# Macaron block on one core: VectorE's order of weight sums, a chunked output projection, and a norm sum one product later

## The chip, the cores and the metric

The kernel runs on one core of a Trainium2 chip. The metric is the device time of one execution in microseconds (us). The engines are TensorE (PE, matrix products; its weight loads are listed as PEld), VectorE (DVE), ScalarE (ACT), GpSimd (POOL) and SyncE (SP), which issues the loads from memory. Each engine works through its own queue in a fixed order and waits for others by semaphores.

## The reference

A transformer block in the macaron form, one batch of 512 tokens, width 1024, in float32:

```python
x = x + 0.5 * swiglu(rmsnorm(x, g1), wg1, wu1, wd1)      # first FFN, hidden 2816
y = rmsnorm(x, g_mix) @ w_in                             # q, k, v, gates of 16 heads
o = concat(moba_attention(8 heads), nsa_attention(8 heads))
x = x + o @ w_out                                        # output projection
x = x + 0.5 * swiglu(rmsnorm(x, g2), wg2, wu2, wd2)      # second FFN
z = rmsnorm(x, gf)
# swiglu(h) = (silu(h @ w_gate) * (h @ w_up)) @ w_down
```

MoBA chooses key blocks of 256 by their mean key; NSA mixes compressed, chosen and windowed keys by three gates. Both add a relative position bias.

## The kernel before

**Layout and precision.** Activations lie transposed: `xs[d]` is block d of 128 features by 512 tokens, d = 0 to 7. A product is made to nearly float32 precision from halves: each operand is split into hi (ACT copies it to the short type) and lo (DVE or POOL subtracts hi), and `mm3` (L99 to L102) issues three matmuls: hi x hi (L100), lo x hi (L101), hi x lo (L102). `halves` (L76 to L96) splits weights into `whi` (L91, ACT) and `wlo` (L95 on DVE, or L93 on POOL).

**FFN.** Class `Ffn` (L187) holds 22 hidden blocks. The first four are "plain": 24 matmuls of 512 columns for gate and 24 for up; `finish` (L281 to L283) multiplies both by R, the reciprocal norm of each token, and `kept` (L250 to L255) splits the result into the halves called `h`. The other 18 go in nine pairs by Winograd's form of Strassen's product: seven products for gate and seven for up, 12 matmuls of 256 columns each. Their weight blocks come as tiles `aw`, sums S1 to S4 of these are made on DVE (`sums`, L303), halves `sph` and `spl` of blocks and sums by `halves_of_x` (L226 ACT, L227 DVE), and the results are put together at L327 to L349 (`t`). The same Strassen form needs sums of the activations (`sums_of_x`, L211 to L224: `xa` to `xd`, halves `th`, `tl`; `blocks_of_x`: `xo`). `down` (L375 to L402) makes the down product of up to four hidden blocks (`pd`), whose banks `half_added` (L487) adds to `x`. `lay` (L411) lists steps and runs each product's loads 12 steps ahead, its sums 6 and its halves 4.

**What sets the order.** A scheduler lays down each engine's order from the program's order and its own model of times; `tc.issue_after(i)` makes it put the instructions of a block behind instruction i on their engine. With `behind_rms = (f, m)` the matmuls of product m of plain block f go behind the matmuls `pr` that sum the squares (L175); `pR` (L181) then hands out the reciprocal norm, and ACT copies it to R (L182).

**Output projection.** It is fill work for the attention: `stream` loads jobs three ahead from a pool of four buffers and PE gets their matmuls between those of the attention. A job of `w_out` (L766 to L778) takes one block d and two of the four pairs of heads. The attention's head leaves its bank `po` by `out_halves` (L805 to L823): ACT copies hi (L819), DVE makes `to` (L820), ACT copies `u` (L822), POOL adds both to lo (L823). The lines of `oT` for pairs 0 to 3 are named `kvn` in the trace.

Of the kernel before, what the change touches and what calls it, by code (L numbers as in the profile page):

```python
# [16 lines left out]
D = 1024  # L17
# [4 lines left out]
FP = 4  # L22
# [7 lines left out]
def block_kernel(ctx: ExitStack, tc: tile.TileContext, A: dict, out: bass.AP):  # L30
# [156 lines left out]
    class Ffn:  # L187
# [14 lines left out]
        def __init__(self, wg, wu, which, tmp, hp, sp):  # L202
            self.w, self.which, self.tmp, self.hp, self.sp = (wg, wu), which, tmp, hp, sp
            self.xg, self.hs, self.steps = None, {}, []
            self.b, self.temps = {}, {}
            self.behind_rms = None
            self.th, self.tl = [sp.tile([128, 4, 3, HT], F32R, name=n, tag=n, bufs=1) for n in ("th3", "tl3")]
            sp.tile([128, 16], F32, name="gap", tag="gap", bufs=1)
# [15 lines left out]

        def halves_of_x(self, hi, lo, v):
            nc.scalar.activation(hi, v, AF.Copy)  # L226
            nc.vector.tensor_tensor(lo, v, f32(hi), ALU.subtract)  # L227

        def blocks_of_x(self, k):
            a, b, c = self.temps.pop(k)  # L230
# [58 lines left out]
        def pair(self, f):  # L289
# [8 lines left out]
            def sums(m, name):  # L298

                a11, a12, a21, a22 = [A[m, i, j] for i in range(2) for j in range(2)]  # L300
                to, x, y, op = {"S1": (a21, a21, a22, ALU.add), "S2": (a11, a21, a11, ALU.add),
                                "S3": (a21, a11, a22, ALU.subtract), "S4": (a12, a11, a12, ALU.add)}[name]
                nc.vector.tensor_tensor(to, x, y, op)  # L303

            def halves_of(m, name):
                i, j = {"A11": (0, 0), "A12": (0, 1), "S1": (1, 0), "S2": (0, 0), "S3": (1, 0), "S4": (0, 1),
# [59 lines left out]
                                  lambda m=m, then=then: then(m)])  # L366
            return steps

        def down(self, w, fs, then, tag="mm", groups=(1,) * NK):

            n = len(fs)
            raw, got, bank = {}, {}, {}

            def loads(d):
                if d % (8 // n) == 0:  # L375
                    raw[d * n // 8] = chunk((8, 128))
                    fetch(raw[d * n // 8], w[d * n // 8])

            def halves_of(d):
                if d % (4 // n) == 0:  # L380
                    i = d * n % 8
                    for k, v in enumerate(halves(raw[d * n // 8][:, i:i + 4])):
                        got[d + k // n, k % n] = v

            def run(d):
                ds = {sum(groups[:g]): range(sum(groups[:g]), sum(groups[:g + 1])) for g in range(len(groups))}.get(d)
                if ds is None:
                    return
                for i in ds:
                    bank[i] = pt(tag, "pd")  # L390
                for ks in ([range(n)] if len(ds) == 1 else [range(n - 1), range(n - 1, n)]):
                    for i in ds:
                        for k in ks:
                            mm3(bank[i], got[i, k], self.hs[fs[k]], k == 0, k == n - 1)
                for i in ds:
                    then(i, bank[i])

            return [[lambda d=d: loads(d), None, lambda d=d: halves_of(d), lambda d=d: run(d), None, True]
                    for d in range(NK)]

# [10 lines left out]
        def lay(self, wd):  # L411

            for f in range(FP):
                self.steps += self.plain(f)
            self.steps += self.down(wd[0], range(FP), half_added, None, (4, 4))
            fills = []
            for f in range(FP, NF, FP):
                fs = range(f, min(f + FP, NF))
                pairs = [step for i in fs[::2] for step in self.pair(i)]
                self.steps += self.mixed(pairs, fills) if fills else pairs  # L420
                if len(fs) == FP:
                    fills = self.down(wd[f // FP], fs, half_added)
# [128 lines left out]
    with ExitStack() as ph:  # L551
# [211 lines left out]
        oT = {}  # L763
        out_done = set()

        def w_out(d, k0, k1):  # L766
            def body(w):
                while any(2 * k + 1 not in out_done for k in range(k0, k1)):
                    yield
                p = pt("mm", "pw")  # L770
                for k in range(k0, k1):
                    mm3(p, w[k - k0], oT[k], k == k0, k == k1 - 1)
                    yield
                nc.vector.tensor_tensor(xs[d], p, xs[d], ALU.add)
                if k1 == 4:
                    got["x", d] = gained(d, 2)
                    squares(tmp, d, "t", 6)
            return A["w_o"][d][:, k0:k1], body  # L778

        def stream(jobs, ahead=3):  # L780

# [24 lines left out]
        def out_halves(h):  # L806
# [13 lines left out]
            nc.vector.tensor_tensor(t[b], o[:64], f32(hi[b]), ALU.subtract)  # L820
            u = tmp.tile([128, S], F32, name="u", tag="t", bufs=6)
            nc.scalar.activation(u[b], o[64:], AF.Copy)  # L822
            nc.gpsimd.tensor_tensor(lo[b], t[b], u[b], ALU.add)  # L823

        QIS = ((0, 1), (2,), (3,))
        JS = ((0,), (1,), (2, 3))
# [143 lines left out]
        for i in range(4):  # L970
            fill += [proj(2 * i, moba_t("q", i)), proj(2 * i + 1, moba_t("k", i))]
            if i == 2:
                fill += [w_out(d, 4, 6) for d in range(NK)]
        fill += [w_out(d, k, k + 2) for k in (6, 0) for d in range(NK)]
        last = [w_out(d, 2, 4) for d in range(NK)]
        work = stream(pre + fill + last)
        done = [0]

# [60 lines left out]
    with ExitStack() as ph:  # L1039
# [2 lines left out]
        sp = ph.enter_context(tc.tile_pool(name="sp3", bufs=2))  # L1042
        ffn = Ffn(A["wg2"], A["wu2"], 2, tmp, hp, sp)
        ffn.xg = xg
        ffn.behind_rms = 1, 0
        hs = ffn.hs

        def after(i):
# [93 lines left out]
def _laid_out(x, norm_ffn1, w_ffn1_gate, w_ffn1_up, w_ffn1_down, norm_mix, w_in, cmp_pos_k, cmp_w1_k,  # L1142
# [19 lines left out]
        "w1": np.stack([kp(cmp_w1_k[0]), kp(cmp_w1_v[0])]),  # L1162
        "w2": np.stack([kp(cmp_w2_k[0]), kp(cmp_w2_v[0])]),
        "pos": c(cat([pos, pos], axis=0)),
        "w_o": _blocks(w_out[0], D, 128),
        "wg2": _blocks(w_ffn2_gate[0], D, 128), "wu2": _blocks(w_ffn2_up[0], D, 128),
        "wd2a": _down(w_ffn2_down[0])[0],
        "wd2b": _blocks(w_ffn2_down[0][F - F % (FP * 128):], F % (FP * 128), S),
# [26 lines left out]
```

## Time and profile before

| | us |
|---|---|
| median of 3 runs | 1009.53 (1008.88 to 1009.92) |
| profiled execution | 1011.25 |
| its span | 1009.5 |
| PE busy | 983.8 |
| DVE busy | 776.9 |
| ACT busy | 564.9 |
| POOL busy | 137.3 |

The span runs from the first to the last instruction of the profiled execution; the rest of its time lies around it. The page's row of PE's granted clock, in tenths for 40 slices, reads 9 in all but the last (8). A busy PE is not a PE at its peak, since matmuls overlap; where PE stands still is seen in the waits and in the starts of its matmuls. The stages in order of time: first FFN to about 360 us, projections and attention to 636, the rest of the output projection to about 655 with the second FFN's first products among it, second FFN and last norm to the end.

### The profile page before, as it was taken

The page shows a single profiled execution, that of the slowest core. Times are in us where ns is not written, and L with a number is a line of the kernel's source. Part 1 is how long each engine was busy: PE and PEld are TensorE (multiplying, and loading weights), DVE is VectorE, ACT ScalarE, POOL GpSimd, SP SyncE. Part 2 cuts the span into 40 slices and gives each one's busy share as a digit, 9 for nine tenths or more (in the row PEclk, how much of TensorE's full clock was granted, in tenths as well). Part 3 has the DMA queues.
Part 4 walks back from the last instruction along what each step waited for, and adds up shares of the span by engine and source line. Part 5 has one row for each costly group of instructions (what it writes and reads, how often), then busy time and mean ns, then how long its engine had stood idle before and what let it go on. Part 6 is the DMA issues. An engine that isn't in the chain of part 4 may idle for free.

```text
span 1009.5 us, 17013 instructions
## 1 busy us (share of the span) xinstructions
PE 983.8 (97%) x6080; PEld 871.0 (86%) x6080; DVE 776.9 (77%) x1578; ACT 564.9 (56%) x1181; POOL 137.3 (14%) x193
## 2 busy tenths in 40 slices
PE   8999999999999999999999999999999999999996
PEld 6779999999999898787878888788899999999995
DVE  6797888788766488758888978779878888776744
ACT  6463654454444266557677977655455445444436
POOL 0000000000000000036555776300000000000002
PEclk9999999999999999999999999999999999999998
DMA  7254544233501125541011322425244232341102
GB/s 244 87 197 153 186 149 113 98 101 89 161 25 54 45 85 177 165 127 38 20 45 32 93 65 84 140 86 209 69 144 142 86 105 91 120 146 43 33 11 84
DMA packets 53513, 104.53 MB, mean 104 GB/s; under 512 B 10513, under 2 KB 19170, under 8 KB 53428
## 3 DMA queue, kind: packets, MB, share of 16 engines
q1 hardware_dynamic: 53428, 103.44, 32.6%
q8 instruction: 48, 0.79, 0.3%
q14 instruction: 37, 0.30, 0.1%
HBM read 97.98 MB, written 5.30 MB: 102 GB/s over the span
## 4 chain that ended last, share of the span: by engine, by line
PE 82%; DVE 11%; DMA 3%; issue 2%; ACT 1%; POOL 0%; SPq 0%; DVEq 0%; ACTq 0%; POOLq 0%
PE pd L102 6%; PE pd L100 6%; PE pd L101 6%; PE pu L100 6%; PE pu L102 5%; PE pu L101 5%; PE pw L100 4%; PE pw L101 4%; PE pw L102 4%; PE pp L102 3%; PE pgu L100 3%; PE pp L100 3%; PE pp L101 3%; PE pgu L101 3%; PE pv L100 3%; PE pgu L102 3%
## 5 line engine op out<-in xcount | busy, mean ns | idle before, releaser
L226 ACT ACTIVATE sph<-aw 128x512 fp32r<-128x512 f32 x252 | 155.7, 628 | 138.0 <-PE pu L101 68.1
L91 ACT ACTIVATE whi<-raw 128x512 fp32r<-128x512 f32 (+2 forms) x216 | 124.6, 589 | 151.3 <-PE pd L101 71.8
L227 DVE TENSOR_TENSOR spl<-aw,sph 128x512 fp32r<-128x512 f32 x252 | 170.0, 685 | 49.5 <-ACT sph L226 47.9
L101 PE MATMUL pd<-h,whi 128*128 128x512 f32 x336 | 131.9, 392 | 1.4 <-DVE h L255 1.4
L102 PE MATMUL pd<-h,wlo 128*128 128x512 f32 x336 | 130.9, 390 | 0.8 <-DVE wlo L95 0.6
L95 DVE TENSOR_TENSOR wlo<-raw,whi 128x512 fp32r<-128x512 f32 (+1 forms) x168 | 110.9, 671 | 23.9 <-ACT whi L91 22.6
L100 PE MATMUL pd<-h,whi 128*128 128x512 f32 x336 | 129.0, 392 | 0.0
L100 PE MATMUL pu<-th,sph 128*128 128x256 f32 x432 | 121.5, 281 | 1.1 <-DVE t L339 1.1
L303 DVE TENSOR_TENSOR aw<-aw 128x512 f32<-128x512 f32 x144 | 97.6, 683 | 31.7 <-DMA aw<-in_wg 13.6
L102 PE MATMUL pu<-th,spl 128*128 128x256 f32 x432 | 121.1, 280 | 0.0
L101 PE MATMUL pu<-tl,sph 128*128 128x256 f32 x432 | 121.0, 280 | 0.0
L487 DVE SCALAR_TENSOR_TENSOR x<-pd,x 128x512 f32<-128x512 f32 x88 | 59.9, 685 | 44.7 <-PE pd L102 44.4
L100 PEld LDWEIGHTS pu<-th,sph 128*128 128x128 f32 x432 | 81.6, 189 | 2.8 <-DVE t L339 1.3
L101 PEld LDWEIGHTS pu<-tl,sph 128*128 128x128 f32 x432 | 81.9, 190 | 1.1
L100 PE MATMUL pw<-xo,sph 128*128 128x256 f32 x288 | 80.8, 281 | 0.8 <-DVE x L487 0.5
L102 PEld LDWEIGHTS pu<-th,spl 128*128 128x128 f32 x432 | 81.2, 188 | 0.1
L101 PE MATMUL pw<-xo,sph 128*128 128x256 f32 x288 | 80.4, 280 | 0.0
L102 PE MATMUL pw<-xo,spl 128*128 128x256 f32 x288 | 79.7, 280 | 0.0
L102 PEld LDWEIGHTS pd<-h,wlo 128*128 128x128 f32 x336 | 63.1, 188 | 14.1 <-DVE wlo L95 1.2
L101 PEld LDWEIGHTS pd<-h,whi 128*128 128x128 f32 x336 | 63.3, 188 | 12.8 <-DVE h L255 2.2
L100 PEld LDWEIGHTS pd<-h,whi 128*128 128x128 f32 x336 | 62.9, 188 | 11.1
L100 PEld LDWEIGHTS pw<-xo,sph 128*128 128x128 f32 x288 | 54.1, 188 | 2.6 <-ACT sph L226 1.6
(245 smaller groups left out, 2454.5 us busy)
## 6 DMA issues: line engine op xcount, KB each, us to landing
aw<-in_wg SPq DMA_DIRECT2D x72, 256.0 KB, 3.8
aw<-in_wu SPq DMA_DIRECT2D x72, 256.0 KB, 3.6
raw<-in_wd1a SPq DMA_DIRECT2D x20, 512.0 KB, 4.7
raw<-in_wd2a SPq DMA_DIRECT2D x20, 512.0 KB, 4.8
raw<-in_w_a SPq DMA_DIRECT2D x16, 512.0 KB, 4.4
raw<-in_w SPq DMA_DIRECT2D x8, 512.0 KB, 3.7
raw<-in_w_o SPq DMA_DIRECT2D x32, 128.0 KB, 2.2
raw<-in_wg SPq DMA_DIRECT2D x7, 512.0 KB, 3.8
```

What stands on the lines that cost most here:

```text
L91: nc.scalar.activation(hi, v, AF.Copy)
L95: nc.vector.tensor_tensor(lo, v, f32(hi), ALU.subtract)
L100: nc.tensor.matmul(p, w[0], v[0], start=first, stop=False, skip_group_check=again)
L101: nc.tensor.matmul(p, w[0], v[1], start=False, stop=False, skip_group_check=again)
L102: nc.tensor.matmul(p, w[1], v[0], start=False, stop=last, skip_group_check=again)
L226: nc.scalar.activation(hi, v, AF.Copy)
L227: nc.vector.tensor_tensor(lo, v, f32(hi), ALU.subtract)
L303: nc.vector.tensor_tensor(to, x, y, op)
L487: nc.vector.scalar_tensor_tensor(xs[d], p, 0.5, xs[d], ALU.mult, ALU.add)
```

## The change

Four edits:

1. `halves_of_x` remembers the last `lo` it issued. The sums S1 to S4 on DVE, and the split of the down weights, go behind the newest one (`behind_lo`). The first down part of each FFN is left out (`kept_back=False`) as far as its weights are concerned.
2. `w_out` takes four blocks and two pairs of heads at a time: 8 jobs with a load of 512 KB and two splits of 128x512 instead of 32 jobs with 128 KB and one split of 128x256. The last two jobs hold four banks (two of tag `mm`, two of `s`) and make the products of pair 2 of all four before those of pair 3. The weights' layout follows.
3. For the last head, 7, the final add of `out_halves` is on DVE instead of POOL.
4. `behind_rms` of the second FFN is (1, 1) instead of (1, 0).

```diff
         def halves_of_x(self, hi, lo, v):
             nc.scalar.activation(hi, v, AF.Copy)
-            nc.vector.tensor_tensor(lo, v, f32(hi), ALU.subtract)
+            self.last_lo = nc.vector.tensor_tensor(lo, v, f32(hi), ALU.subtract)
+
+        def behind_lo(self):
+            return tc.issue_after(self.last_lo.ins) if self.last_lo else nullcontext()
...
-                nc.vector.tensor_tensor(to, x, y, op)
+                with self.behind_lo():
+                    nc.vector.tensor_tensor(to, x, y, op)
...
-        def down(self, w, fs, then, tag="mm", groups=(1,) * NK):
+        def down(self, w, fs, then, tag="mm", groups=(1,) * NK, kept_back=True):
...
-                    for k, v in enumerate(halves(raw[d * n // 8][:, i:i + 4])):
+                    with self.behind_lo() if kept_back else nullcontext():
+                        parts = halves(raw[d * n // 8][:, i:i + 4])
+                    for k, v in enumerate(parts):
...
-            self.steps += self.down(wd[0], range(FP), half_added, None, (4, 4))
+            self.steps += self.down(wd[0], range(FP), half_added, None, (4, 4), False)
...
-        def w_out(d, k0, k1):
+        def w_out(g, k0, last=False):
             def body(w):
-                while any(2 * k + 1 not in out_done for k in range(k0, k1)):
+                while any(2 * k + 1 not in out_done for k in (k0, k0 + 1)):
                     yield
-                p = pt("mm", "pw")
-                for k in range(k0, k1):
-                    mm3(p, w[k - k0], oT[k], k == k0, k == k1 - 1)
+                ps = {}
+                for i, k in [(i, k) for k in range(2) for i in range(4)] if last else [
+                        (i, k) for i in range(4) for k in range(2)]:
+                    if k == 0:
+                        ps[i] = pt("mm" if not last or i < 2 else "s", "pw")
+                    mm3(ps[i], w[2 * i + k], oT[k0 + k], k == 0, k == 1)
                     yield
-                nc.vector.tensor_tensor(xs[d], p, xs[d], ALU.add)
-                if k1 == 4:
-                    got["x", d] = gained(d, 2)
-                    squares(tmp, d, "t", 6)
-            return A["w_o"][d][:, k0:k1], body
+                    if k == 1:
+                        d = 4 * g + i
+                        nc.vector.tensor_tensor(xs[d], ps[i], xs[d], ALU.add)
+                        if last:
+                            got["x", d] = gained(d, 2)
+                            squares(tmp, d, "t", 6)
+            return A["w_o"][k0 // 2, g], body
...
-            nc.gpsimd.tensor_tensor(lo[b], t[b], u[b], ALU.add)
+            (nc.vector if h == 7 else nc.gpsimd).tensor_tensor(lo[b], t[b], u[b], ALU.add)
...
-                fill += [w_out(d, 4, 6) for d in range(NK)]
-        fill += [w_out(d, k, k + 2) for k in (6, 0) for d in range(NK)]
-        last = [w_out(d, 2, 4) for d in range(NK)]
+                fill += [w_out(g, 4) for g in range(2)]
+        fill += [w_out(g, k) for k in (6, 0) for g in range(2)]
+        last = [w_out(g, 2, True) for g in range(2)]
...
-        ffn.behind_rms = 1, 0
+        ffn.behind_rms = 1, 1
```

The change shifts the lines: of the new kernel, L228 is L227 of before, L309 is L303, L260 is L255, L288 is L283, L218, L219 and L221 are L217, L218 and L220, L495 is L487, L788 is L774, L834 and L838 are L820 and L823.

What the edits do to the order, at three places. First, DVE in the first FFN, ahead of the `h` of the fourth plain block; before:

```order
L283 TENSOR_TENSOR t<-t 128x512
L303 TENSOR_TENSOR aw<-aw 128x512
L217 TENSOR_TENSOR xc<-xa 128x256
L227 TENSOR_TENSOR xo<-xa,xo 128x256
L303 TENSOR_TENSOR aw<-aw 128x512
L227 TENSOR_TENSOR xo<-xb,xo 128x512
L255 TENSOR_TENSOR h<-t,h 128x512
```

And now:

```order
L288 TENSOR_TENSOR t<-t 128x512
L218 TENSOR_TENSOR xc<-xa 128x256
L228 TENSOR_TENSOR xo<-xa,xo 128x256
L228 TENSOR_TENSOR xo<-xb,xo 128x512
L219 SCALAR_TENSOR_TENSOR xd<-xc,xb 128x256
L221 TENSOR_TENSOR xa<-xb,xa 128x256
L228 TENSOR_TENSOR spl<-aw,sph 128x512 x2
L309 TENSOR_TENSOR aw<-aw 128x512
L228 TENSOR_TENSOR spl<-aw,sph 128x512
L260 TENSOR_TENSOR h<-t,h 128x512
```

The sums (`aw<-aw`) have gone from between the block sums, two more of them from just above these rows; three `spl`, one sum and two pieces of `sums_of_x` stand ahead of `h` that stood behind it.

Second, PE after the last matmul of the attention (`po`); before, `kvn_7522` is the lo of the last pair of heads, which `out_halves` makes last:

```order
L107 MATMUL po_7529<-tl_7514,vm_4844 128x128
L100 MATMUL pw_7764<-kvn_7421,whi_7718 128x512
L101 MATMUL pw_7764<-kvn_7422,whi_7718 128x512
L102 MATMUL pw_7764<-kvn_7421,wlo_7719 128x512
L100 MATMUL pw_7783<-kvn_7421,whi_7732 128x512
L101 MATMUL pw_7783<-kvn_7422,whi_7732 128x512
L102 MATMUL pw_7783<-kvn_7421,wlo_7733 128x512
L100 MATMUL pw_7764<-kvn_7521,whi_7718 128x512
L100 MATMUL pw_7783<-kvn_7521,whi_7732 128x512
L101 MATMUL pw_7764<-kvn_7522,whi_7718 128x512
```

Now six matmuls of another block follow the last `po`, then these rows; `kvn_7510` is the lo of the last pair:

```order
L100 MATMUL pw_7676<-kvn_7409,whi_7562 128x512
L101 MATMUL pw_7676<-kvn_7410,whi_7562 128x512
L102 MATMUL pw_7676<-kvn_7409,wlo_7563 128x512
L100 MATMUL pw_7676<-kvn_7509,whi_7562 128x512
L100 MATMUL pw_7684<-kvn_7509,whi_7566 128x512
L100 MATMUL pw_7688<-kvn_7509,whi_7566 128x512
L100 MATMUL pw_7680<-kvn_7409,whi_7562 128x512
L101 MATMUL pw_7680<-kvn_7410,whi_7562 128x512
L102 MATMUL pw_7680<-kvn_7409,wlo_7563 128x512
L100 MATMUL pw_7680<-kvn_7509,whi_7562 128x512
L101 MATMUL pw_7676<-kvn_7510,whi_7562 128x512
```

Eight matmuls stood between the last `po` and the first that needs the last lo; sixteen stand there now, in four banks. On DVE the last lo is made here, behind an `x` add and the `wlo` of the second FFN's first weights:

```order
L834 TENSOR_TENSOR to<-po,kvn 64x512
L788 TENSOR_TENSOR x_91<-pw,x_91 128x512
L95 TENSOR_TENSOR wlo<-raw,whi 128x512
L838 TENSOR_TENSOR kvn<-to,u 64x512
L788 TENSOR_TENSOR x_72<-pw,x_72 128x512
```

Before, `kvn<-to,u` stood on POOL, with nothing of another kind behind `to` on DVE but the next `x` adds.

Third, DVE in the second FFN around the `h` of the fourth plain block and the first add of the down part; before:

```order
L303 TENSOR_TENSOR aw<-aw 128x512
L218 SCALAR_TENSOR_TENSOR xd<-xc,xb 128x256
L220 TENSOR_TENSOR xa<-xb,xa 128x256
L227 TENSOR_TENSOR spl<-aw,sph 128x512 x4
L227 TENSOR_TENSOR xo<-xc,xo 128x256
L255 TENSOR_TENSOR h<-t,h 128x512
L219 SCALAR_TENSOR_TENSOR xd<-xd,xb 128x256
L227 TENSOR_TENSOR tl_7919<-xa,th_7918 128x256
L303 TENSOR_TENSOR aw<-aw 128x512 x2
L227 TENSOR_TENSOR spl<-aw,sph 128x512
L227 TENSOR_TENSOR tl_7919<-xd,th_7918 128x512
L487 SCALAR_TENSOR_TENSOR x_72<-pd,x_72 128x512
```

And now:

```order
L260 TENSOR_TENSOR h<-t,h 128x512
L219 SCALAR_TENSOR_TENSOR xd<-xc,xb 128x256
L221 TENSOR_TENSOR xa<-xb,xa 128x256
L228 TENSOR_TENSOR spl<-aw,sph 128x512 x2
L309 TENSOR_TENSOR aw<-aw 128x512
L228 TENSOR_TENSOR spl<-aw,sph 128x512
L309 TENSOR_TENSOR aw<-aw 128x512
L228 TENSOR_TENSOR xo<-xc,xo 128x256
L228 TENSOR_TENSOR spl<-aw,sph 128x512
L220 SCALAR_TENSOR_TENSOR xd<-xd,xb 128x256
L495 SCALAR_TENSOR_TENSOR x_72<-pd,x_72 128x512
```

The `spl` and the sums have gone from ahead of `h` to behind it, and stand between `h` and the first `x`.

## Rows read from the trace of the kernel before

**Rows 1.** The page: busy time, share of the span and number of instructions of each engine; then the chain of work that ended last, its shares by engine.

```profile
PE 983.8 (97%) x6080; PEld 871.0 (86%) x6080; DVE 776.9 (77%) x1578; ACT 564.9 (56%) x1181; POOL 137.3 (14%) x193
...
PE 82%; DVE 11%; DMA 3%; issue 2%; ACT 1%; POOL 0%; SPq 0%; DVEq 0%; ACTq 0%; POOLq 0%
```

**Rows 2.** Timeline of PE in the first down part: start, duration (of all that are grouped), engine, line, operation, number, and in brackets the idle time before it and what ended it.

```profile
67.30 1.07 PE L100 MATMUL pd<-h,whi 128*128 128x512 f32 x4
68.69 0.50 PE L101 MATMUL pd<-h,whi 128*128 128x512 f32 x1 [0.32 <-DVE h L255]
```

**Rows 3.** Waits of PE from 60 to 105 us: what waited for what, us in total, times, longest.

```profile
PE pu L100 <- DVE t L339: 1.1, 1, 1.1
PE pd L102 <- DVE wlo L95: 0.6, 1, 0.6
PE pw L100 <- DVE x L487: 0.5, 1, 0.5
PE pd L101 <- DVE h L255: 0.3, 1, 0.3
```

**Rows 4.** Waits of PE from 636 to 650 us.

```profile
PE pw L101 <- POOL kvn L823: 1.6, 1, 1.6
PE pw L100 <- DVE x L774: 0.8, 2, 0.5
```

**Rows 5.** Waits of PE from 700 to 800 us.

```profile
PE pd L101 <- DVE h L255: 1.1, 1, 1.1
PE pv L100 <- ACT sph L226: 0.9, 1, 0.9
PE pv L102 <- DVE spl L227: 0.3, 1, 0.3
PE pw L100 <- ACT sph L226: 0.3, 1, 0.3
PE pu L100 <- DVE t L348: 0.3, 1, 0.3
```

**Rows 6.** Timeline of DVE in the first FFN, 60.5 to 75 us.

```profile
61.20 0.67 DVE L303 TENSOR_TENSOR aw<-aw 128x512 f32<-128x512 f32 x1
...
66.76 0.67 DVE L303 TENSOR_TENSOR aw<-aw 128x512 f32<-128x512 f32 x1
...
67.96 0.67 DVE L255 TENSOR_TENSOR h<-t,h 128x512 fp32r<-128x512 f32 x1
...
72.31 1.27 DVE L487 SCALAR_TENSOR_TENSOR x<-pd,x 128x512 f32<-128x512 f32 x2
73.51 0.67 DVE L95 TENSOR_TENSOR wlo<-raw,whi 128x512 fp32r<-128x512 f32 x1
```

**Rows 7.** The page's DMA issues: tile and source, queue, number, KB each, us from issue to landing.

```profile
raw<-in_w_a SPq DMA_DIRECT2D x16, 512.0 KB, 4.4
...
raw<-in_w_o SPq DMA_DIRECT2D x32, 128.0 KB, 2.2
```

**Rows 8.** Groups of POOL's instructions by form: line, operation, shape, number, busy us, mean ns of one, idle before and its releasers.

```profile
L93 POOL TENSOR_TENSOR wlo<-raw,whi 128x256 fp32r<-128x256 f32 x32 | 24.8, 780 | 10.6 <-ACT whi L91 9.1 <-PE pw L101 1.1
L93 POOL TENSOR_TENSOR wlo<-raw,whi 128x512 fp32r<-128x512 f32 x16 | 21.2, 1324 | 4.0 <-ACT whi L91 4.0
```

**Rows 9.** Timeline of all engines at the end of the attention, 636 to 640 us.

```profile
636.00 0.28 PE L107 MATMUL po<-tl,vm 128*128 128x128 f32 x1
...
636.31 0.59 ACT L819 ACTIVATE kvn<-po 64x512 fp32r<-64x512 f32 x1 [0.17 <-PE po L107]
...
637.01 0.68 DVE L820 TENSOR_TENSOR to<-po,kvn 64x512 f32<-64x512 f32 x1 [0.41 <-POOL wlo L93]
...
637.73 0.59 ACT L822 ACTIVATE u<-po 64x512 f32<-64x512 f32 x1 [0.82 <-DVE to L820]
638.46 1.26 POOL L823 TENSOR_TENSOR kvn<-to,u 64x512 fp32r<-64x512 f32 x1 [1.49 <-ACT u L822]
...
639.77 0.50 PE L101 MATMUL pw<-kvn,whi 128*128 128x512 f32 x1 [1.60 <-POOL kvn L823]
```

**Rows 10.** One line of DVE, L595, a subtraction of two tensors in SBUF: number, duration in ns (least, median, most), first and last start. POOL has no work from 389 to 439 us and has from 521 to 607.

```profile
L595 DVE TENSOR_TENSOR ak<-t,ak x8: 690/946/1673, 521.5 to 607.3; 64x512 fp32r<-64x512 f32 x8
L595 DVE TENSOR_TENSOR kvn<-t,kvn x4: 676/686/691, 389.2 to 438.6; 64x512 fp32r<-64x512 f32 x4
```

**Rows 11.** Timeline of PE in the second FFN: the products that hand on the reciprocal norm.

```profile
667.20 0.60 PE L181 MATMUL pR<-ident,rc 128*128 128x128 f32 x4
```

**Rows 12.** Timeline of DVE in the second FFN, from the first use of R to the first add of the down part.

```profile
668.46 1.29 DVE L281 TENSOR_TENSOR t<-pgu,R 128x512 f32<-128x512 f32 x2 [2.15 <-ACT R L182]
...
707.15 0.68 DVE L255 TENSOR_TENSOR h<-t,h 128x512 fp32r<-128x512 f32 x1
...
710.83 0.68 DVE L487 SCALAR_TENSOR_TENSOR x<-pd,x 128x512 f32<-128x512 f32 x1
```

**Rows 13.** Busy time by engine in the stretch of the first FFN in which its R is made: stretch and length, then busy us (and instructions) of PE, PEld, DVE, ACT and POOL, granted clock of PE, DMA share, GB/s.

```profile
20.00:45.00 25.00, 25.00 (x110) 18.54 (x110) 18.35 (x34) 10.38 (x17) 0.00 (x0) 1.00 0.34 108
```

**Rows 14.** Waits of DVE from 690 to 800 us.

```profile
DVE aw L303 <- DMA aw<-in_wg: 5.6, 3, 4.2
```

**Rows 15.** Waits of PE from 440 to 636 us, the two largest.

```profile
PE ps_s L864 <- DVE m L870: 1.1, 6, 0.2
PE ps_t L888 <- DVE th L949: 1.0, 1, 1.0
```

More of the change, by code (lines that the diff above doesn't have):

```diff
@@ L205, in __init__ @@
             self.b, self.temps = {}, {}
+            self.last_lo = None
             self.behind_rms = None
@@ L1164, in _laid_out @@
         "pos": c(cat([pos, pos], axis=0)),
-        "w_o": _blocks(w_out[0], D, 128),
+        "w_o": c(w_out[0].reshape(4, 2, 128, 2, 4, 128).transpose(0, 3, 2, 4, 1, 5)).reshape(4, 2, 128, 8, 128),
         "wg2": _blocks(w_ffn2_gate[0], D, 128), "wu2": _blocks(w_ffn2_up[0], D, 128),
```

## The prediction

> **What bounds the kernel now.** I read the busy shares and the chain first: TensorE (PE) is busy 97% of the span and carries 82% of the chain, VectorE (DVE) 11% [rows 1]. So nothing can be won but the moments in which PE stands still, and these I took stretch by stretch from the waits of PE. A wait costs a little more than the idle time that the view gives. Four products of 512 columns start from 67.30, together 1.07 us, the last one 0.39, so they start 0.227 us apart; the next would start at 68.21 and starts at 68.69, which is 0.48 for an idle time of 0.32 [rows 2]. I add 0.16 us to each wait. The stretches that the change reorders then hold: first FFN, 60 to 105 us, 2.5 idle + 4 x 0.16 = 3.1 us [rows 3]; the end of the attention, 636 to 650 us, 2.4 + 3 x 0.16 = 2.9 [rows 4]; second FFN, 700 to 800 us, 2.9 + 5 x 0.16 = 3.7 [rows 5]. That is 9.7 us, 1% of the time: the ceiling, unless the attention stretch moves too.
>
> The profiled execution took 1011.25 us, 1009.5 of it span; the median of the runs is 1009.53. All terms are differences inside the span, and I take them off the median.
>
> **Sums behind the halves (first FFN).** No work is added: 144 sums before and after, at the same size. Only DVE's order moves. Before, four sums (the first at 61.20, the last at 66.76) stand ahead of `h` at 67.96, for which PE waits 0.3, and four `spl` and more stand ahead of the adds `x` at 72.31 and the half `wlo` at 73.51, for which it waits 0.5 and 0.6 [rows 3, 6]. In the new order the four are gone from there, but three `spl`, one sum and two block operations have come ahead of the same `h`. DVE's instructions follow each other 0.60 us apart at 512 columns (two steps from 66.76 to 67.96 [rows 6]) and, by an estimate from half the columns, 0.34 at 256. From `xa` up to `h` that makes 7.4 us of work in the new order against 6.7 before: `h` comes 0.7 later, and its wait grows from 0.5 to 1.2. The first add comes about 0.3 and the first `wlo` about 0.9 earlier, so of 0.7 + 0.8 us I leave 0.6. The wait of 1.1 + 0.16 for `t` of L339 (PE must have a bank emptied by it) I take as gone: DVE's order has that `t` 3 us earlier. Sum: -0.7 + 0.9 + 1.27 = **1.5 us gained**, between 0 (`t` is held by something else) and 3.1.
>
> That the first down part is exempt costs nothing that I can find: its `wlo` keep their places, four steps ahead. The other down parts' `wlo` move 17 to 30 us later in DVE's order, still four steps before their product; the DVE gaps in the pairs hide them.
>
> **Output projection in chunks of four blocks.** The products are the same (192 of 512 columns). Thirty-two loads of 128 KB (2.2 us) become eight of 512 KB (4.4 for the same size from `w_a`) [rows 7], three jobs ahead of use, at 24 x 0.227 = 5.4 us of products per job: hidden, and if it were not, one load late is 4.4 at most once. GpSimd's (POOL) halves go from 32 x 0.780 = 24.8 us to 16 x 1.324 = 21.2 [rows 8].
>
> The term lies at the end. After the last `po` (636.00) the chain is 0.59 on ScalarE (ACT), 0.68 on DVE, 0.59 on ACT, 1.26 on POOL, and PE starts at 639.77 [rows 9]. Before, eight products (1.8 us) stand in between; now sixteen (16 x 0.227 = 3.6), since two jobs hold four banks and start on what is ready. With the last add on DVE (0.68 by the first row of its kind, below) the chain ends at 639.77 - 1.26 + 0.68 = 639.2 if nothing is in its way. Something is: an `x` add and a `wlo` of the next weights stand ahead of it on DVE, the second of them behind a `whi` that ACT does between its two pieces. The add's bank is full at about 637.6, add and `wlo` take DVE to 638.9, the last add ends at 639.6, PE can go on at about 639.7 and wants to at 636.00 + 17 x 0.227 = 639.86. So the 1.76 us go, with 0.15 to spare. The two waits for a bank (0.8 + 0.32) go as well: a bank is wanted 1.6 us after its last product, and an add takes 0.68. Ends: 2.9 if all goes, 1.7 if the chain is 1.2 later. I take **2.6 us**.
>
> What the last add costs on DVE: the same line, shape and operands (two inputs in SBUF, 64x512) took 676 to 691 ns where POOL had no work and 690 / 946 / 1673 (least, median, most) where it had [rows 10]. I take 0.68, as POOL's queue has only one half of `w_out` left there; 0.95 would cost 0.1 us of stall, 1.67 about 0.85. The Trainium skill (GPSIMD Engine Reference, Specifications) says that GpSimd's SBUF interfaces are shared with VectorE and that instructions of VectorE with two SBUF inputs contend with it. The trace agrees (946 against 686). By that rule the add would take the median under load, since a `wlo` on POOL falls near it, and the sum would lose 0.1 us; without it nothing.
>
> **Norm sum of the second FFN one product later.** Nothing is added (4 + 4 small products). `pR`, which hands R on, starts at 667.20 [rows 11]; it and the sum before it now stand 5.2 us (23 products) later among PE's products, and R with them. DVE had R at 668.46, reached `h` at 707.15 and the first `x` at 710.83 [rows 12]: 38.7 and 42.4 us. In the new order the work between R and `h` is 7.0 us less (sums and `wlo` moved out of it), so `h` is 7.0 - 5.2 = 1.8 us earlier against PE, and its wait of 1.1 + 0.16 goes. But the first `x`, which empties the bank for the first pair's product, has only 6 us less ahead of it, and PE, no longer held at `h`, comes 1.24 earlier: I find it 1.2 us late. Gain against new wait: **0**, between -1.3 and +1.3. The first FFN has its norm sum at this later place already, and PE is busy without a break from 20 to 45 us there [rows 13]: the place by itself costs no bank.
>
> **The pairs of the second FFN.** Four waits remain (0.9, 0.3, 0.3, 0.3, with 0.16 each 2.4 us) [rows 5], for `sph`, `spl` and `t`. DVE stood 5.6 us, in three pieces up to 4.2, at sums whose gate weights had not landed [rows 14], with everything behind it waiting. Where the sum is kept behind the halves, less stands behind it: the `spl` come 3 to 5 us earlier in DVE's order, against waits of 1. I take 2.0 of the 2.4: **2.0 us**, between 0 and 2.4 (the same loads may just be late).
>
> **The attention stretch, 440 to 636 us.** It is reshuffled by the larger chunks; its two largest waits of PE, 1.1 (six of 0.2 and less) and 1.0, end on DVE [rows 15]. The edit gives them no less work and no more. **0**, within 1.3 either way (those two, give or take).
>
> Sum: 1.5 + 2.6 + 0 + 2.0 + 0 = 6.1; 1009.5 - 6.1 = **1003.4 us**. Its own range goes from 1000.5 to 1006.5.
>
> **Rivals.**
> 1. *The later norm sum costs more than it frees.* R is 5.2 us later and all of DVE's work in that stretch hangs on it (it idled 2.15 us for R [rows 12], which it can't fill). If DVE is 2 us later than I count, `h` waits 2.0 - 0.65 = 1.35 and `x` 1.2 + 0.65 = 1.85 on top, 3.2 where 1.24 was: 1003.4 + 2.0 = 1005.4. For it: my margin at `h` is 0.65 us in 34. Against: 7 us less work.
> 2. *The wide halves get in the attention's way and the gains in the pairs don't come.* A POOL half is 1.324 where it was 0.780 [rows 8]: 0.54 more ahead of a scaled `lp`, 16 times, 8.7 us at worst. With a fifth of that lost (1.7), nothing from the first FFN and half of the other two terms (2.3): 1009.5 + 1.7 - 2.3 = 1008.9. The Trainium skill (Perfetto Trace Analysis, Optimizing Scalar/DVE Operations) speaks for this rival: engines that are not full but cause bubbles elsewhere should rather break instructions up. No row shows a wait of PE in that stretch that ends on a half [rows 15]; by the rule the time is that of this rival.
> 3. *Slower: the sums come too late.* A sum kept behind the newest `lo` runs 3 to 8 us later on DVE, where six steps of twelve products ahead of need are some 8 us (an estimate, at half the 0.227 of 512 columns). Behind it ACT must make `sph` and DVE `spl`. Where fewer than about 2 us (0.6 + 0.7, as such pieces take in [rows 9], and the way between) are left, PE waits, as it does once already (0.9 + 0.16 for `sph`) [rows 5]; and `spl` frees the weight buffers, so the next loads start later. Once in each of the eight pairs of the touched stretches: 8 x 1.06 = 8.5, with the gains of the FFNs lost: 1009.5 - 2.6 + 8.5 = 1015.4. It decides when the sums' lead falls under 2 us. Against: DVE is idle for 23% of the span [rows 1], and by my count the nearest sum keeps about 3 us.
>
> **How the numbers follow.** Forecast 0.50, rival 1 0.20, rival 2 0.18, rival 3 0.12. A measurement tells about 0.2%, 2 us, from no change, so faster is below 1007.5: the forecast, rival 1 and a third of rival 2, 0.76; same: the rest of rival 2, 0.12; slower: 0.12. Range: the best ends added (3.1 + 2.9 + 3.7 + 1.3 of the attention's waits = 11.0) give 998.5; the poor ends of the terms, and rival 2 with a little over, 1009.5. Rival 3 lies outside.
>
> **What would show it.** First FFN: `h` of the fourth block waits about 1.2, no wait for `t` of L339's kind near 98 us. End of the attention: POOL is not in the chain, PE goes from the last `po` to the second FFN with under 0.3 us of waiting, no wait for `x` of the output projection. Second FFN: no wait at `h`, one of about 1.2 at the first add of the down part. Pairs: no wait over 0.5 on `sph`. It would be wrong if waits of PE for `sph` or `spl` come up pair after pair, or if the attention stretch has new waits behind wide halves.

## The result and the profile after

| | before | after |
|---|---|---|
| median, us | 1009.35 (4 runs) | 1003.74 (4 runs, 1002.51 to 1003.96) |
| ratio | | 0.9947, 95% interval 0.9935 to 0.9959 |
| profiled execution, us | 1011.25 | 1003.62 |
| its span, us | 1009.5 | 1001.8 |

5.6 us less; 6.1 had been forecast. The spans of the two profiled executions differ by 7.7, but that of before came from an execution 1.9 us above its median.

Waits of PE after, in the stretches of rows 3, 4 and 5: 60 to 105 us; none at all from 625 to 650 and from 650 to 700; 700 to 800 us.

```profile
PE pd L101 <- DVE h L260: 1.0, 1, 1.0
...
PE pu L100 <- DVE x L495: 1.2, 1, 1.2
PE pu L100 <- ACT t L351: 0.4, 1, 0.4
```

Of four waits in the first FFN one is left, that for `h`, which grew from 0.3 to 1.0 [rows 3]. The three at the end of the attention are gone [rows 4]. In the second FFN the wait for `h` has become one for the first add `x`, and of the four in the pairs a short one is left [rows 5].

The timeline of DVE in the first FFN shows why `h` waits longer: three `spl` and a sum stand in front of it.

```profile
65.58 1.27 DVE L228 TENSOR_TENSOR spl<-aw,sph 128x512 fp32r<-128x512 f32 x2
66.79 0.67 DVE L309 TENSOR_TENSOR aw<-aw 128x512 f32<-128x512 f32 x1
67.39 0.67 DVE L228 TENSOR_TENSOR spl<-aw,sph 128x512 fp32r<-128x512 f32 x1
67.99 0.67 DVE L260 TENSOR_TENSOR h<-t,h 128x512 fp32r<-128x512 f32 x1
```

The end of the attention, all engines, from the last `po` on (answers to rows 9):

```profile
632.94 0.28 PE L107 MATMUL po<-tl,vm 128*128 128x128 f32 x1
...
633.26 0.59 ACT L833 ACTIVATE kvn<-po 64x512 fp32r<-64x512 f32 x1 [1.67 <-PE po L107]
...
633.95 0.69 DVE L834 TENSOR_TENSOR to<-po,kvn 64x512 f32<-64x512 f32 x1 [0.41 <-ACT kvn L833]
...
634.51 0.64 ACT L91 ACTIVATE whi<-raw 128x512 fp32r<-128x512 f32 x1 [0.66 <-PE pw L101]
634.70 0.69 DVE L788 TENSOR_TENSOR x<-pw,x 128x512 f32<-128x512 f32 x1
...
635.17 0.59 ACT L836 ACTIVATE u<-po 64x512 f32<-64x512 f32 x1
...
635.31 0.68 DVE L95 TENSOR_TENSOR wlo<-raw,whi 128x512 fp32r<-128x512 f32 x1
636.02 0.69 DVE L838 TENSOR_TENSOR kvn<-to,u 64x512 fp32r<-64x512 f32 x1
...
636.86 0.47 PE L101 MATMUL pw<-kvn,whi 128*128 128x512 f32 x1
```

The lo is done at 636.71, 3.77 us after the last `po` started, and PE takes it up at 3.92 without a break. The forecast was 3.6 to 3.7 against a need at 3.86.

DVE's waits from 690 to 800 us no longer name the weight sums at all [rows 14]; the first is

```profile
DVE spl L228 <- ACT sph L227: 8.3, 9, 2.3
```

In the attention stretch (440 to 636 us) PE's idle time went from 4.3 to 4.7 us over all rows of the view: a wait for `tl` at 600 us is new, one of 0.8 for `t` of a projection is gone. The two largest now, where rows 15 show those of before:

```profile
PE ps_t L903 <- DVE th L964: 1.3, 2, 1.0
PE ps_t L903 <- DVE tl L907: 1.2, 1, 1.2
```

The new wait comes from the wide halves. One of `w_out` runs on POOL when DVE starts `aq`, an operation that takes 0.69 us otherwise:

```profile
597.46 1.29 POOL L93 TENSOR_TENSOR wlo<-raw,whi 128x512 fp32r<-128x512 f32 x1
597.60 1.69 DVE L596 TENSOR_TENSOR aq<-t,aq 64x512 fp32r<-64x512 f32 x1
...
601.48 0.41 PE L903 MATMUL ps_t<-ident,lpn 128*128 128x128 f32 x2 [1.15 <-DVE tl L907]
```

DVE has hardly a break from there to `tl`, so without the 1.00 us the wait would be about 0.15 (an estimate). In all ten traces with the chunks this `aq` takes 1.69 to 1.72 us; before and in e1, e9 and e14, which have the narrow halves, it takes 0.69.

### The profile page after: what moved, and what is told of

Read it like the earlier page. It is cut to its first block, busy times and chain, and to the rows that moved or that the text cites. A ratio compares the mean times of both kernels' runs of the same rounds, so it can differ in the third digit from the quotient of the medians.

```text
span 1001.8 us, 16901 instructions
## 1 busy us (share of the span) xinstructions
PE 981.3 (98%) x6080; PEld 871.6 (87%) x6080; DVE 780.9 (78%) x1579; ACT 566.8 (57%) x1165; POOL 132.2 (13%) x176
## 4 chain that ended last, share of the span: by engine, by line
PE 87%; DVE 7%; DMA 2%; ACT 2%; issue 2%; SPq 0%; ACTq 0%; DVEq 0%
PE pd L102 7%; PE pd L100 7%; PE pd L101 7%; PE pu L100 6%; PE pu L101 6%; PE pu L102 6%; PE pw L100 4%; PE pw L102 4%; PE pw L101 4%; PE pp L102 3%; PE pp L100 3%; PE pp L101 3%; PE pgu L100 3%; PE pv L100 3%; PE ps_t L903 3%; PE pgu L101 3%
## 5 line engine op out<-in xcount | busy, mean ns | idle before, releaser
L227 ACT ACTIVATE sph<-aw 128x512 fp32r<-128x512 f32 x252 | 157.7, 630 | 151.8 <-PE pu L101 65.8
L91 ACT ACTIVATE whi<-raw 128x512 fp32r<-128x512 f32 (+1 forms) x200 | 122.0, 621 | 176.4 <-PE pd L101 93.6
L228 DVE TENSOR_TENSOR spl<-aw,sph 128x512 fp32r<-128x512 f32 x252 | 170.6, 685 | 56.6 <-ACT sph L227 53.8
L309 DVE TENSOR_TENSOR aw<-aw 128x512 f32<-128x512 f32 x144 | 98.1, 682 | 0.0
L495 DVE SCALAR_TENSOR_TENSOR x<-pd,x 128x512 f32<-128x512 f32 x88 | 59.8, 684 | 36.5 <-PE pd L102 35.5
```

The lines of the kernel that those rows point to most:

```text
L228: self.last_lo = nc.vector.tensor_tensor(lo, v, f32(hi), ALU.subtract)
L495: nc.vector.scalar_tensor_tensor(xs[d], p, 0.5, xs[d], ALU.mult, ALU.add)
```

## The experiments

The medians stand beside runs of the kernel before that were taken with them (1008.75 to 1009.61 us). Single executions of one kernel spread by 1 to 7 us (the kernel before from 1005.8 to 1013.1), so a difference of about 1 us between two kernels isn't settled by the medians; there the waits of PE are the better witness.

| run | median, us (runs) | ratio to before, 95% |
|---|---|---|
| e1 sums alone | 1003.25 (6) | 0.9936 (0.9918 to 0.9954) |
| e2 chunks and last add alone | 1010.09 (12) | 1.0015 (1.0002 to 1.0028) |
| e3 norm sum at its old place | 1005.02 (8) | 0.9955 (0.9940 to 0.9970) |
| e15 all but the sums | 1008.58 (12) | 0.9999 (0.9988 to 1.0011) |
| e5 last add on GpSimd | 1003.41 (6) | 0.9942 (0.9923 to 0.9960) |
| e9 last add alone | 1009.00 (10) | 1.0003 (0.9988 to 1.0017) |
| e6 two banks | 1005.42 (10) | 0.9970 (0.9959 to 0.9980) |
| e7 first down part kept too | 1015.72 (4) | 1.0074 (1.0058 to 1.0089) |
| e10 four halves on GpSimd | 1013.06 (5) | 1.0046 (1.0033 to 1.0059) |
| e11 first pair kept behind | 1001.98 (6) | 0.9932 (0.9914 to 0.9950) |
| e14 sums, first pair kept behind | 1003.86 (6) | 0.9949 (0.9931 to 0.9967) |
| e16 the new kernel again | 1002.14 (5) | 0.9938 (0.9921 to 0.9955) |

**e1: the first edit alone.** Before, with the edit of `halves_of_x`, `sums` and `down`, nothing else.

> The kernel before with the first edit alone (sums and down halves behind the newest lo; output projection, last add and norm sum as before). Theory (the gains are local to each edit and add up): the waits of both FFNs go, about 2.5 us in the first and 3 in the second, since R is not later here and the wait for the first add x of the second FFN does not come; the 2.9 us at the end of the attention stay. About 1004.5 us, 1003.5 to 1006. Rival (moving the sums only shifts waits and the output projection brings the gain): 1007.5 or more, with PE waits for sph or spl in the pairs.

1003.25 us, the whole of the change's gain. Waits of PE, 60 to 130 and then 625 to 800 us:

```profile
PE pd L101 <- DVE h L259: 1.0, 1, 1.0
...
PE pw L101 <- POOL kvn L830: 1.6, 1, 1.6
PE pw L100 <- DVE x L781: 0.8, 2, 0.5
PE pu L100 <- ACT t L350: 0.6, 1, 0.6
```

The FFNs' waits are as expected, the waits at the attention's end untouched, and no wait for `x` stands in the second FFN. By waits (0.16 added to each) the FFNs went from 3.1 + 3.7 to 1.2 + 0.8, 4.8 us; the time moved by 6.1 (interval 4.6 to 8.3). The 3.1 of the first FFN is that of one execution; other traces with the old order have up to 5.4 there (under e15), which can hold the rest. e1 moves the sums and the halves of the down weights together; what each of them brings wasn't run.

**e2: chunks and last add alone.**

```diff
-                with self.behind_lo():
-                    nc.vector.tensor_tensor(to, x, y, op)
+                nc.vector.tensor_tensor(to, x, y, op)
...
-                    with self.behind_lo() if kept_back else nullcontext():
+                    with nullcontext():
...
-        ffn.behind_rms = 1, 1
+        ffn.behind_rms = 1, 0
```

> The new kernel without the first and fourth edits: chunks of four blocks and the last add on VectorE, sums in the old order, norm sum at its old place. Theory: the 2.9 us of waits at the end of the attention go, those of the FFNs stay (3 and 3.5 us), and PE waits about 1 us at the norm sum, which now comes before the squares are summed: 1007.0 us, 1006 to 1008. Rival: the projection's chunks bring most of the gain: 1005 or less.

1010.09, no gain and perhaps a loss, worse than either theory. The attention's end is without waits, as expected. But at the norm sum PE waits 2.0, not 1, and then runs slow, as the next run shows best.

**e3: the norm sum back at its old place.** One line, `behind_rms = 1, 0`, in the new kernel.

> The new kernel with the norm sum of the second FFN at its old place (1, 0). Theory (the later place frees nothing and costs the 1.2 us wait for x): that wait goes, but PE waits about 1 us for the sum of squares at the norm sum instead: 1003.5 us, 1003 to 1004. Rival 1 of the prediction (the later R is what holds VectorE back): 1002.4, without a new wait. Third: the early norm sum stalls by more than it frees, 1005 or more.

1005.02, the third case. First the last squares (`acc`) and the norm sum (`pr`) before; then both in e3, with PE's timeline; then e3's windows by engine (columns as in rows 13):

```profile
658.94 1.47 DVE L164 TENSOR_TENSOR acc<-acc,sq 128x512 f32<-128x512 f32 x2
661.26 0.95 PE L175 MATMUL pr<-ones_f,acc 128*128 128x1 f32 x8
```

```profile
656.16 0.39 PE L102 MATMUL pgu<-xo,wlo 128*128 128x512 f32 x1
...
657.78 0.69 DVE L164 TENSOR_TENSOR acc<-acc,sq 128x512 f32<-128x512 f32 x1
658.52 1.05 PE L175 MATMUL pr<-ones_f,acc 128*128 128x1 f32 x8 [1.98 <-DVE acc L164]
...
660.46 0.63 PE L101 MATMUL pgu<-xo,whi 128*128 128x512 f32 x1
660.88 0.63 PE L102 MATMUL pgu<-xo,wlo 128*128 128x512 f32 x1
```

```profile
655.00:660.00 5.00, 3.02 (x18) 2.33 (x17) 3.37 (x7) 2.70 (x4) 0.00 (x0) 1.00 0.62 186
660.00:665.00 5.00, 5.00 (x16) 3.94 (x15) 0.74 (x2) 0.63 (x1) 0.00 (x0) 0.66 0.06 23
```

Counted from the start of the last `po` (636.00 before, 634.24 in e3), PE is at the norm sum 22.3 us later in e3 and 25.3 before, since its waits in the projection are gone; the last squares end 24.2 us later in e3 and 24.4 before. VectorE has become no faster, and PE waits 2.0 for it: most of the 2.9 won just ahead. Behind that wait PE's clock is at the lower of its two levels (1.2 GHz) for part of the next 5 us, granted 0.66 on average: the matmuls follow each other 0.43 us apart instead of 0.227, and some 8 of them cost 1.6 us more. The fourth edit, which wasn't run alone, is what makes the second bearable: this wait goes, and PE pays 1.2 for `x` instead.

**e15: all but the sums.** The first two pieces of e2's diff, with the norm sum at (1, 1).

> The new kernel without the first edit: chunks, last add on VectorE and the later norm sum, with the sums in the old order. Theory (rival 1 of the prediction in full: without the 7 us of work that the first edit takes out from between R and h, the 5.2 us later R makes h late): PE waits 4 to 6 us at h in the second FFN, with 1 to 2 us of lower clock behind it, and the waits of the first FFN stay: 1011 to 1014 us. Other theory (the scheduler puts h first anyway, the later norm sum is harmless by itself): 1007 to 1008.

1008.58: my theory fell, and the time is a little above the other theory's. PE waits 1.0 for `h` in the second FFN, not 4 to 6: DVE's order was laid down anew for the later R. PE's waits from 690 to 800 us:

```profile
PE pd L101 <- DVE h L260: 1.0, 1, 1.0
PE pu L100 <- DVE t L344: 1.0, 1, 1.0
PE pv L100 <- ACT sph L227: 0.8, 1, 0.8
PE pu L100 <- DVE x L494: 0.4, 1, 0.4
PE pd L100 <- ACT h L259: 0.4, 1, 0.4
```

4.4 us here with the 0.16s, 0.7 more than before, and 0.4 more in the attention: 1.1 of the 2.9 at its end are given back. The first FFN (60 to 130 us) has 3.8, but that isn't the edits' doing: the order of DVE and PE is that of before up to the attention, and with this order the traces have 3.1 (before), 3.8 (here), 4.3 (e2) and 5.4 (e9). With the first edit the change, e16, e1, e3, e5 and e6 all have 1.2. So by the waits edits two to four bring about 1.8 us without the first, and the time shows nothing (0 within 1.2 us); where the rest goes isn't shown.

**e5 and e9: the last add alone.** In e5 the new kernel has `nc.gpsimd` again for head 7; in e9 the kernel before has `nc.vector` for it.

> The new kernel with the last add of the attention back on GpSimd; PE's order is the same. Theory: u ends at 635.8, the add takes 1.28 to 637.2, PE wants to go on at 636.8: a wait of about 0.45, 1004.2 us. Rival (two-input additions of VectorE and GpSimd get in each other's way, so that it is the same or better off GpSimd's side): no wait, 1003.7 or less.

> The kernel before with the last add of the attention on VectorE alone. Theory: the chain behind the last po gets shorter by 1.26 - 0.68 = 0.6 us and the wait of 1.6 becomes 1.0; the banks' waits stay: 1008.8 us, the same within what can be told. Rival (the additions contend, or VectorE has the x adds in front): the wait stays at 1.6 or grows, 1009.4.

Both waits came as expected, of e5 first (630 to 650 us), then of e9:

```profile
PE pw L101 <- POOL kvn L838: 0.3, 1, 0.3
```

```profile
PE pw L101 <- DVE kvn L823: 1.0, 1, 1.0
```

0.47 with the 0.16 for e5, 0.6 less than before for e9; neither can be told in the time. On DVE the add took 0.69 us; the two halves of `w_out` on POOL ran at other moments.

**e6: two banks.**

```diff
-                for i, k in [(i, k) for k in range(2) for i in range(4)] if last else [
-                        (i, k) for i in range(4) for k in range(2)]:
+                for i, k in [(i, k) for i in range(4) for k in range(2)]:
...
-                        ps[i] = pt("mm" if not last or i < 2 else "s", "pw")
+                        ps[i] = pt("mm", "pw")
```

> The new kernel with its last two projection jobs one block after the other in the two banks of tag mm, as before. Theory (the four banks give PE the sixteen products that cover the chain of the last lo): with eight products or so in between, PE waits about 1.2 us for the lo and again about 0.5 for a bank, 1.5 to 2 us in all at the end of the attention: 1005.3 us, 1004.5 to 1006. Rival (the chunk's larger pieces do it, not the banks): under 0.5 us of waits there, 1003.7.

The time is as the theory had it, 1005.42, the reason is not. At the attention's end only 0.2 + 0.3 are waited; the two largest waits of the stretch from 625 to 800 us lie in the second FFN:

```profile
PE pd L101 <- DVE h L260: 1.9, 1, 1.9
PE pu L100 <- ACT t L351: 1.6, 1, 1.6
```

So without the four banks two thirds of what the attention's end gave are still there (2.9 to 0.8 with the 0.16s); the larger loss is at `h`. From its first use of R to that `h` DVE has 71 instructions and 36.3 us in e6, 62 and 31.7 in the change; four `spl` and two sums stand ahead of `h` again. Why the scheduler's order came out so isn't shown.

**e7: the exemption taken away.** `False` became `True` in the call of the first `down`.

> The new kernel without the exemption: the first down part's weight halves are kept behind the newest lo too. Theory: the wlo of the first down part then come late for its first products, PE waits for wlo at the start of the down part in both FFNs, 0.5 to 2 us in all: 1004.2 to 1005.7 us. Rival (VectorE has less ahead of h, which comes earlier by as much): 1003 or less, the wait for h in the first FFN under 0.6.

1015.72, 12 us slower than the change and far over the theory's 2, on another wait than it named. Waits of PE from 60 to 105 and from 690 to 800 us:

```profile
PE pd L101 <- DVE h L260: 4.2, 1, 4.2
PE pd L100 <- ACT h L259: 0.5, 1, 0.5
...
PE pd L100 <- ACT h L259: 1.2, 1, 1.2
PE pd L102 <- DVE wlo L95: 0.3, 1, 0.3
```

With the `wlo` late, the products that need them were laid behind those that need `h`. PE comes to `h` 2 us earlier, DVE makes it 1 us later (68.99 for 67.99), and there is nothing else to do: 4.2 in each FFN, with the lower clock behind it. The exemption, which I had priced at nothing, carries the change.

**e10: halves on GpSimd.** To take DVE's load off `h` and `x`:

```diff
             def halves_of(m):
+                side[0] = f == 3
                 got[m] = halves(got[m])
+                side[0] = False
```

> The new kernel with the four wlo of the fourth plain block on GpSimd in each FFN, where GpSimd is idle. VectorE has 4 x 0.60 = 2.4 us less ahead of h and of the first x. Theory (VectorE's backlog alone sets those two waits): the wait for h in the first FFN (1.0) and for x in the second (1.2) go or fall under 0.3: 1001.7 us, 1001 to 1002.5. Rival (the shared interface of the two engines: VectorE's two-input operations run longer beside GpSimd's and eat the relief): waits of 0.6 and more stay, 1003 to 1004.

1013.06, 9 us slower. DVE in the first FFN, where a POOL half runs from 36.07 for 3.11 us; then the durations of the two lines that form sums of `x` (least, median, most) of the whole run, and POOL's halves from 30 to 60 us by form:

```profile
36.01 0.74 DVE L216 SCALAR_TENSOR_TENSOR xa<-x,gcol,R 128x512 f32<-128x512 f32 x1
36.67 0.68 DVE L290 TENSOR_TENSOR t<-t 128x512 f32<-128x512 f32 x1
...
37.94 1.78 DVE L216 SCALAR_TENSOR_TENSOR xb<-x,gcol,R 128x512 f32<-128x512 f32 x1
```

```profile
L216 DVE SCALAR_TENSOR_TENSOR xa<-x,gcol,R x8: 737/740/1787, 32.1 to 697.8; 128x512 f32<-128x512 f32 x8
L216 DVE SCALAR_TENSOR_TENSOR xb<-x,gcol,R x8: 734/740/1787, 33.2 to 690.9; 128x512 f32<-128x512 f32 x8
```

```profile
L93 POOL TENSOR_TENSOR wlo<-raw,whi 128x512 fp32r<-128x512 f32 x4 | 9.6, 2401 | 36.2 <-ACT whi L91 36.2
```

In the first FFN four of DVE's operations grew, three of them from 0.74 to 1.78 and one to 1.18, 3.6 us for the 2.4 saved; POOL's took 2.4 each where they take 1.3 [rows 8]. PE then waits 3.7 for `h` in both FFNs, with the lower clock behind. The contention is not all of it. In the first FFN `h` comes 2.0 us later than in the change (70.02 for 67.99): 1.2 are the 3.6 less 2.4, about 1.5 are a sum, an `spl` and an `xo` more ahead of it, and R comes 0.7 earlier; PE is there 0.7 earlier as well. The rival held in its mechanism, not in its size (1003 to 1004): DVE is busy for the whole 38 us from 32 to 70 in both kernels, with 69 instructions here and 75 in the change.

**e11 and e14: the first pair behind `h` and `x`.**

The lines that remember `h` and `x` are left out here:

```diff
-                with self.behind_lo():
+                with self.behind_lo(), tc.issue_after(self.x_ins[0].ins) if f == FP else nullcontext():
                     nc.vector.tensor_tensor(to, x, y, op)
...
-                self.halves_of_x(hi, lo, A[m, i, j])
+                with tc.issue_after(self.h_ins[FP - 1].ins) if f == FP else nullcontext():
+                    self.halves_of_x(hi, lo, A[m, i, j])
```

e11 is the new kernel with these lines, e14 the kernel before with them and the first edit; e16 is the new kernel once more.

> The new kernel with the first pair's spl and sums of each FFN kept behind the h of the fourth plain block, and its sums also behind the first add x, so that the two waits that are left have no one in front. In VectorE's order h stands 2.4 us earlier in the first FFN and x 1.2 us earlier in the second. Theory (VectorE's order alone sets these two waits): both go (1.0 and 1.2 us, with 0.16 each 2.5), and no wait for sph or spl takes their place: 1001.5 us, 1000.5 to 1002.5. Rival (the first pair's halves are then late): PE waits for spl at the first pair, 1003.5 or more.

> The kernel before with the first edit and with the first pair's spl and sums behind h and x as in the run above; projection, last add and norm sum as before. Theory (the second to fourth edits give 2.9 at the end of the attention and cost the wait for x, which the order takes away): 1002.1 us by the waits alone (1003.25 of the first edit alone less the 1.15 of h), so 0.5 or more slower than the run above. Rival (the second to fourth edits give nothing even then): as fast as the run above or faster.

> The new kernel once more, so that differences of 1 to 2 us between it and the runs above rest on more executions, with a second profile. Theory (the waits for h of the first FFN and x of the second are a matter of order, the same in each execution): both are there again, 1.0 and 1.2 us; the median is 1003.4 to 1004, so that the run with the first pair kept behind is 1.5 to 2 us faster. Rival (that difference is scatter between executions): 1002.5 or less.

The waits for `h` and (but for 0.2) `x` went, but others came. Waits of PE of e11, 60 to 105 and 700 to 800 us:

```profile
PE pd L102 <- DVE wlo L95: 0.6, 1, 0.6
PE pw L100 <- ACT sph L228: 0.3, 1, 0.3
...
PE pv L100 <- ACT sph L228: 0.5, 1, 0.5
PE pv L100 <- DVE x L497: 0.2, 1, 0.2
```

2.2 us with the 0.16s, where the change has 3.1 in the same stretches (2.5 in e16). e11 is at 1001.98; the change itself, run again in e16, came to 1002.14 with its two waits unchanged (1.0 and 1.2). So the lead of e11 is scatter as far as these runs tell, and so is e14's lag. No version clearly beats the change; the first edit alone (e1) and e11 can't be told from it.

## Why the prediction was right

The time (1003.4 for 1003.74) and the terms, read as waits with 0.16 each, before and after:

- **First FFN**, 1.5 forecast: 3.1 to 1.2, 1.9 us. `h` grew by 0.7 as counted, `t` of L339 went; of `x` and `wlo`, of which 0.6 was left standing in the sum, only 0.09 is left. Against the other traces with the old order the gain is 2.6 to 4.2.
- **Attention's end**, 2.6 forecast: 2.9 to 0. The chain came out to a tenth. The last add took 0.69, not the 0.95 of a shared interface, and POOL's half didn't meet it.
- **Norm sum**, 0 forecast: 1.24 for `h` against 1.36 for `x`, the 1.2 of idle time that was forecast. The numbers that the prediction gives for it don't make 1.2, though: 6 us less work, R 5.2 later and PE 1.24 earlier leave 0.44. In the trace DVE takes 37.2 us from its first use of R (667.53) to the first add (704.75) where it took 42.4 [rows 12]. That is 5.2 less, so `x` gained nothing on PE. The size was right, the working shown for it was not.
- **Pairs**, 2.0 forecast: 2.4 to 0.56, 1.8.
- **Attention stretch**, 0 forecast: 0.4 lost. "No less work and no more" was wrong: the wide half costs a wait of 1.15 + 0.16, and the wait of 0.8 that went makes up for most of it.

Together 1.9 + 2.9 - 0.1 + 1.8 - 0.4 = 6.1, where 5.6 was measured (interval 4.1 to 6.6).

What the sum hid is to whom it belongs. By the prediction's terms the first edit would bring 1.5 + 2.0 and the 1.26 at `h`, 4.8 together, and the other three 2.6 less the 1.2 at `x`, about 1.3. The times give 6.1 to the first edit (e1, interval 4.6 to 8.3) and none that can be told to the other three (e15: 0 within 1.2); the change isn't told from e1. So that the total came out as near is in part luck. The projection's 2.9 is real in the trace, and by the waits more than half of it is given back: the squares come no earlier with the chunks, so the norm sum must move so that PE doesn't wait 2.0 and slow down (e3), the later R costs the wait for `x`, which neither e1 nor e3 has (1.36), and a wide half costs a wait in the attention (0.4 net). I booked the gain at `h` under the fourth edit, but the first brings it with R at its old place (e1, e3), and I never asked what that old place would cost behind the chunks. "The exemption costs nothing" was true and empty: without it the change loses (e7).

Rival 1 was half right: its wait for `x` came, at the size of the forecast. Rival 2's mechanism showed in small: no wait of PE ends on a wide half itself, but the one at 600 us ends on VectorE's work that such a half held up, 0.4 us net for the 1.7 that the rival had put on it. The Trainium skill (Perfetto Trace Analysis, Optimizing Scalar/DVE Operations) says of ScalarE and VectorE that breaking instructions up may let work end sooner when they cause bubbles elsewhere; no run here has narrow halves in the new order, so whether that would take this wait away isn't shown. Rival 3 didn't come: the sums' lead held. The Trainium skill's rule on the shared interface, by which VectorE's instructions with two SBUF inputs contend with GpSimd (GPSIMD Engine Reference, Specifications), had no place at the last add. In e10 and at `aq` the trace agrees: 1.78 us for 0.74 and 1.69 for 0.69.

## What to carry to other kernels

Where one engine's order decides, look for work that waits for a transfer (here the sums of weights) ahead of work that someone needs, and put the first behind the second; with PE 97% busy a few us of its waits were all there was to win. Price an edit at the place where it acts and then follow the next common point (here the norm sum), where a gain upstream turns into a wait. Moving work from VectorE to an idle GpSimd can cost VectorE more than it saves, and a longer piece on GpSimd can hold up VectorE's work beside it.

## What the runs showed of the hardware

- After a wait of 2.0 us (e3) PE ran at 1.2 GHz for about 3 us: 0.63 us a matmul for 0.39, 0.43 apart for 0.227. After 3.7 us (e10, from 70 us) and 4.2 (e7, from 70 us) the granted clock was 0.50 as well. But after 2.4 us in e9 (98 to 100 us) and 1.9 in e6 it stayed at 1.00, as after the 1.0 and 1.2 of the change. And after two waits of 0.87 and 0.55 us at 408 us it fell in the trace of the change and not in that of e16, the same program, whose span is 2.0 us shorter. In the lines below the granted clock is the third figure from the end, 0.50 against 1.00. So the length of a wait alone didn't decide whether the clock fell, and two executions of one program can differ by it: some 1.7 us here, an estimate from the granted clock from 409 to 415 us.
- In the change and in e10, operations of VectorE with two inputs in SBUF that took longer beside a two-input operation of GpSimd ended 0.54 to 0.56 us after GpSimd's at 512 columns, 0.28 at 256, whatever the operation: `xb` (`scalar_tensor_tensor`) took 1.78 us for 0.74, `aq` 1.69 for 0.69, `h` in the second FFN of e10 1.70 for 0.67. At other moments GpSimd's was the one that waited: its half at 36.07 in e10 took 3.11 us for 1.29, while four two-input operations of VectorE beside it kept their 0.41 to 0.74.

The stretch from 411 to 413 us (columns as in rows 13) in the change, then in e16:

```profile
411.00:413.00 2.00, 2.00 (x8) 1.61 (x7) 1.33 (x3) 0.63 (x1) 0.00 (x0) 0.50 0.77 205
```

```profile
411.00:413.00 2.00, 2.00 (x14) 1.77 (x13) 1.46 (x3) 1.29 (x3) 0.00 (x0) 1.00 0.71 195
```
